# Down projections of a two-layer encoder: nine of sixteen feature pairs by a seven-product scheme in three groups, the last weights kept in SBUF

## The chip, the core and the metric

The kernel runs on one core of a Trainium2 chip. A core has a matrix engine (TensorE, PE in the profile; its weight loads are shown as PEld), a vector engine (VectorE, DVE), a scalar engine (ScalarE, ACT), a general engine (GpSimd, POOL) and a queue engine that only issues DMAs (SyncE, SP). They work from two on-chip memories, SBUF and PSUM (where matmuls accumulate, in eight banks), and each engine runs its own list of instructions in order, held up only by semaphores. DMA brings data from and to the chip's main memory. The metric is the device time of one execution, in microseconds, as the median of several runs; lower is better.

## What is computed

The reference is a trunk of two transformer layers, applied with the same weights to a batch of 512 tokens and one of 256, model width 1024, feed-forward width 4096, all in 32-bit floats. Layer 0 mixes neighbourhood attention and grouped-query attention, layer 1 is differential attention; each is followed by a squared-ReLU feed-forward block, and a norm ends the trunk:

```python
for layer in range(DEPTH):
    ...
    h = rmsnorm(x, ln_mlp[layer])
    x = x + jnp.square(jax.nn.relu(h @ w_up[layer])) @ w_down[layer]
return rmsnorm(x, ln_f)
```

The change is about the last product of each layer, `H @ w_down` with `H` of 768 tokens by 4096 features, called the down projection below.

## The kernel before

**Layout.** Activations are kept transposed: a tile has 128 features on the partitions and all 768 tokens (`NT`) along the free axis, the 512 tokens of one request first, the 256 of the other behind. `x`, the residual stream, is eight such tiles. `HT` is half the tokens, 384.

**Split operands.** A 32-bit product is made of three matmuls in the `fp32r` type: each operand is split into a high part, a copy rounded by ScalarE, and a low part, the rest, by a VectorE subtraction (`halve` for activations, lines 113 to 120; `wsplit` for weights, lines 77 to 82), and high x high, high x low and low x high are summed in PSUM. `wtile` loads a weight tile (three `wraw` buffers, by SP's queue) and splits it into `whi` and `wlo` (four buffers each).

**The feed-forward block** is `mlp` (line 798). The up projection already works by a seven-product scheme for 2 x 2 blocks of (128 output features) x (512 input features) x (384 tokens): `weights` loads a block pair and has POOL form four sums of weight blocks (line 866), `second` forms the sums of activations once (lines 822 to 838), `product` (line 874) issues 12 matmuls of 384 columns for each of the seven products, and VectorE adds the results into `z` (line 889 and its neighbours). `finish` applies norm, ReLU and square and writes each pair of 128 features, `H[mp]`, to DRAM; there are sixteen pairs in a layer.

**The down projection** follows (lines 960 to 991). It runs in `NG` = 4 groups of `GF` = 8 feature tiles, that is, four pairs. For each group `read` (line 919) loads a pair of `H` into an `hr` tile (two buffers, issued on POOL's queue, line 922) and splits it into two `hp` tiles. Then, for each of four output pairs `mq`, two weight tiles are loaded and split, and for each of two output tiles `m`, `proj_feat` (line 195, its matmul on line 204) issues 8 x 3 x 2 matmuls: eight feature tiles, three terms, and two pieces of the tokens, of 512 columns (`dna`, a bank with the tag `mm`) and 256 columns (`dnb`, tag `at`). VectorE adds the two banks to `x[m]` (line 982). There are three `mm` and five `at` banks.

The last group of layer 1 is `final` (line 769): it runs over the 512-token piece and then over the 256-token piece, loading and splitting the group's eight weight tiles for each piece anew, and after each piece it does the last norm (`rstd`, `spread`), scales the eight tiles by `R` on VectorE and POOL (line 795) and writes the output. In layer 0 the last group also splits the new `x` for the next layer and sums its squares.

**What sets the order.** The kernel is written for a tile framework that follows the program's dependencies, hands out buffers of each tag, places the semaphores, and arranges each engine's list of instructions when the kernel is built: an instruction written later may be placed earlier where its inputs and buffers allow. On the chip the order of each engine's list is then fixed.

## Time and profile before

| what | value |
|---|---|
| median of 3 runs | 1823.96 us (1821.44 to 1826.17) |
| the profiled execution's own time | 1822.1 us |
| its span in the profile | 1820.1 us |
| mean granted clock of TensorE | 0.992 |
| first down projection's matmuls | from 621.2 to 892.7 us |
| second down projection, `final` included | from 1533.8 to 1809.2 us |

The profile is one execution. A row of a group of instructions gives source line, engine, operation, output and input by the program's names, shapes and count, then the busy time and the mean duration of one, then the idle time of that engine just before these instructions and what ended it. Matmuls overlap one another, so that a matmul's duration is longer than the distance between two starts. Timeline rows give the start in microseconds from the span's start, the duration, and the instruction. A line number can be that of a helper: line 81 is the low part of any weight, line 117 that of any activation without a gain.

### The profile page before, as it was taken

How to read it: one execution, taken by the hardware profiler on the slowest of the kernel's cores; microseconds unless marked ns; L12 is line 12 of the kernel's file. 1: busy time of each engine (PE TensorE's matmuls, PEld its weight loads, DVE VectorE, ACT ScalarE, POOL GpSimd, SP SyncE). 2: the span in 40 equal slices, each digit the busy share in tenths (PEclk: the TensorE clock that was granted, in tenths of full speed). 3: DMA queues.
4: the chain of work that ended last, by engine and by line, in shares of the span. 5: the costliest groups of instructions: out<-in, count | busy, mean ns of one | idle time of the engine just before them, and what ended most of it. 6: DMA issues, size and time to landing. Idle time of an engine off the chain costs nothing.

```text
span 1820.1 us, 28502 instructions
## 1 busy us (share of the span) xinstructions
PE 1777.1 (98%) x11358; PEld 1627.3 (89%) x11358; DVE 1127.7 (62%) x2083; ACT 764.2 (42%) x1485; POOL 363.5 (20%) x366
## 2 busy tenths in 40 slices
PE   7999999999999999999999999999989999999997
PEld 7877888899999988888999999988989999888877
DVE  7777647497766634325366776775976667343255
ACT  6665534364434412213235555554544334122143
POOL 1421000014544200000022222210235442000002
PEclk8999999999999999999999999999999999999999
DMA  5111222313333634323211110122133336343233
GB/s 166 44 33 37 68 83 88 131 35 110 139 125 130 213 111 139 119 67 122 93 51 44 47 48 22 53 68 93 36 109 140 122 125 207 126 131 124 70 99 115
DMA packets 50019, 176.70 MB, mean 97 GB/s; under 512 B 5856, under 2 KB 8672, under 8 KB 49888
## 3 DMA queue, kind: packets, MB, share of 16 engines
q1 hardware_dynamic: 38656, 121.91, 21.2%
q0 software_dynamic: 4608, 25.17, 4.1%
q10 hardware_dynamic: 6624, 27.81, 3.9%
q8 instruction: 89, 1.46, 0.3%
q14 instruction: 42, 0.34, 0.1%
HBM read 142.63 MB, written 31.46 MB: 96 GB/s over the span
## 4 chain that ended last, share of the span: by engine, by line
PE 78%; DVE 8%; issue 8%; DMA 3%; ACT 3%; POOL 1%; DVEq 0%; SPq 0%; ACTq 0%; POOLq 0%
PE up L881 23%; PE dna L204 11%; PE dqk L192 8%; PE dnb L204 6%; PE opa L204 5%; PE dvp L192 4%; PE fin L786 3%; DMA hr<-H 2%; PE opb L204 2%; PE npa L204 2%; PE ds L270 2%; PE dpv L713 2%; DVE t L815 1%; PE vp L192 1%; PE qp L192 1%
## 5 line engine op out<-in xcount | busy, mean ns | idle before, releaser
L881 PE MATMUL up<-c,whi 128*128 128x384 f32 x1824 | 468.6, 338 | 5.8 <-ACT whi L80 5.8
L881 PEld LDWEIGHTS up<-c,whi 128*128 128x128 f32 x1824 | 331.9, 189 | 6.6 <-ACT whi L80 6.5
L204 PE MATMUL dna<-hp,whi 128*128 128x512 f32 x896 | 331.8, 394 | 1.1 <-DVE hp L117 0.9
L80 ACT ACTIVATE whi<-wraw 128x1024 fp32r<-128x1024 f32 (+2 forms) x200 | 193.3, 967 | 324.5 <-PE dnb L204 222.6
L881 PE MATMUL up<-c,wlo 128*128 128x384 f32 x912 | 308.1, 339 | 2.1 <-DVE wlo L81 2.1
L81 DVE TENSOR_TENSOR wlo<-wraw,whi 128x1024 fp32r<-128x1024 f32 (+2 forms) x204 | 228.4, 1121 | 98.9 <-ACT whi L80 98.7
L204 PE MATMUL dnb<-hp,whi 128*128 128x256 f32 x896 | 250.0, 283 | 0.0
L204 PEld LDWEIGHTS dna<-hp,whi 128*128 128x128 f32 x896 | 168.1, 188 | 42.1 <-DVE hp L117 1.9
L866 POOL TENSOR_TENSOR s<-wraw 128x512 f32<-128x512 f32 x56 | 94.1, 1699 | 414.9 <-DMA wraw<-in_w_up_dram 199.8
L204 PE MATMUL dna<-hp,wlo 128*128 128x512 f32 x448 | 176.6, 394 | 0.0
L881 PEld LDWEIGHTS up<-c,wlo 128*128 128x128 f32 x912 | 172.2, 189 | 2.9 <-DVE wlo L81 2.9
L204 PEld LDWEIGHTS dnb<-hp,whi 128*128 128x128 f32 x896 | 167.2, 188 | 0.3
L889 DVE TENSOR_TENSOR z<-up,z 128x384 f32<-128x384 f32 x168 | 92.9, 553 | 90.4 <-PE up L881 79.0
L982 DVE TENSOR_TENSOR x<-dna,x 128x512 f32<-128x512 f32 x56 | 38.7, 691 | 165.6 <-PE dna L204 165.4
L204 PE MATMUL dnb<-hp,wlo 128*128 128x256 f32 x448 | 126.9, 283 | 0.0
L192 PE MATMUL dqk<-whi,xh 128*128 128x256 f32 x384 | 114.7, 299 | 0.0
L192 PE MATMUL dqk<-whi,xl 128*128 128x256 f32 x384 | 107.5, 280 | 0.0
L192 PE MATMUL dqk<-wlo,xh 128*128 128x256 f32 x384 | 107.2, 279 | 0.0
L922 POOL DMA_DIRECT2D hr<-H x32 | 17.6, 550 | 431.6 <-DVE hp L117 390.8
L204 PEld LDWEIGHTS dna<-hp,wlo 128*128 128x128 f32 x448 | 84.1, 188 | 18.3
L80 ACT ACTIVATE whi<-s 128x1024 fp32r<-128x1024 f32 x56 | 59.5, 1063 | 84.8 <-PE up L881 83.5
L116 ACT ACTIVATE hp<-hr 128x768 fp32r<-128x768 f32 x64 | 50.9, 837 | 100.2 <-PE dnb L204 61.8
(214 smaller groups left out, 3892.7 us busy)
## 6 DMA issues: line engine op xcount, KB each, us to landing
wraw<-in_w_down_dram SPq DMA_DIRECT2D x72, 512.0 KB, 3.6
wraw<-in_w_up_dram SPq DMA_DIRECT2D x64, 512.0 KB, 3.5
H<-z ACTq DMA_DIRECT2D x32, 768.0 KB, 3.3
hr<-H POOLq DMA_DIRECT2D x32, 768.0 KB, 5.9
wraw<-in_w_in_o_dram SPq DMA_DIRECT2D x24, 512.0 KB, 3.6
wraw<-in_w_in_e_dram SPq DMA_DIRECT2D x16, 512.0 KB, 3.7
x<-in_xT_dram SPq DMA_DIRECT2D x16, 384.0 KB, 5.4
nbias<-in_bias_dram SPq DMA_DIRECT2D x20, 256.0 KB, 3.8
```

The source lines that it names most:

```text
L80: nc.scalar.activation(hi, raw, AF.Copy)
L81: nc.vector.tensor_tensor(out=lo, in0=raw, in1=hi.bitcast(F32), op=ALU.subtract)
L116: nc.scalar.activation(hi, src, AF.Copy)
L192: nc.tensor.matmul(ps[:, :256], st[:, tk], col(k, part, 0, 256), start=(k == 0 and i == 0), stop=(k == KD - 1 and i == 2))
L204: nc.tensor.matmul(ps[:, : e - s], w, mv[:, s:e], start=(k == 0 and i == 0), stop=(k == nk - 1 and i == 2))
L270: nc.tensor.matmul(out[h], q(a_, hp, qs), k(b_, hp, ks), start=i == 0, stop=i == 2)
L713: nc.tensor.matmul(pv, pt[:, i * P : (i + 1) * P], v[:, k0 // P + i, vc], start=(i == 0), stop=(i == nk - 1))
L786: nc.tensor.matmul(ps, lhs(k, part), mv[:, sl], start=(k == 0 and j == 0), stop=(k == GF - 1 and j == 2))
L866: nc.gpsimd.tensor_tensor(out=d_, in0=x_, in1=y_, op=ALU.add)
L881: nc.tensor.matmul(ps, part[a_][:, base + k * P : base + (k + 1) * P], t[:, b_], start=q + k + i == 0, stop=q == n - 1 and k == 3 and i == 2)
L889: nc.vector.tensor_tensor(out=out, in0=x_, in1=y_, op=op)
L982: evac_halves(pa, pb, lambda ps, s: nc.vector.tensor_tensor(out=xm[:, s], in0=ps, in1=xm[:, s], op=ALU.add))
```

## The change

Each down projection is cut by a plan of pairs: 2 plain, 3 by the seven-product scheme, 2 plain, 3, 1 plain, 3, 2 plain. The plain stretches work as before, with stretches of two pairs or one in place of four.

In a group of three pairs, each pair is a 2 x 2 block (two feature tiles by two token halves), and with two output tiles `q` (a 2 x 2 block of weights) gives seven products of 384 columns, each summed over the three pairs (`SJ`). `pair` loads a pair of `H`, forms four sums of its blocks on VectorE, and splits seven operands: three of 384 columns (`small`, buffers `c3`) and two of 768 columns that hold two operands each (`large`, buffers `c6`); `slot` hands out twelve of the first and eight of the second in turn. `down_weights` loads two weight tiles of 768 columns, has POOL form four sums, and splits four tiles. `down_pair` issues the products in the order 1, 2, 6, 5, 7, 3, 4 into three banks: `u` collects products 1, 6, 7 and 4, `v` collects 5 and 3, `r` holds 2. Between the products VectorE adds the current content of a bank to a half tile of `x` or subtracts it, seven times, and the next product goes on accumulating in the same bank. Weights are laid out for this on the host.

`H` is loaded by SP's queue in halves into four buffers of the tag `h`, which the block operands `c0` of the up projection used before. The two temporary weight sums of the up projection get a pool of their own (`us`), which is closed in the last step of the up projection; the sums of the down projection take a spare `x` tile (`sa`) and a tile in `pa_` (`sb`). In layer 0 the pool of split tiles for the next layer is opened after the last group of three.

`final` now has the plan's last stretch, two pairs. Its four weight tiles are loaded and split in the first token piece and kept for the second.

```diff
+SJ = 3
+PLAN = ((2, 0), (3, 1), (2, 0), (3, 1), (1, 0), (3, 1), (2, 0))
...
-        start = woff["w_down"]
         acc = cpool.tile([P, NT], F32, tag="acc", name="acc", bufs=1)
         R = cpool.tile([P, NT], F32, tag="R", name="R", bufs=1)
+        kept = []
         for i, (s, e) in enumerate(SEGS):
-            woff["w_down"] = start
             sl = slice(s, e)
             nm = Norm(sq, (s, e), acc)
             for mq in range(KD // 2):
-                ws = [wtile("w_down", 1024) for _ in range(2)]
+                if i == 0:
+                    kept.append([wtile("w_down", 1024)])
+                ws = kept[mq]
                 for mi in range(2):
                     m = 2 * mq + mi
                     ps = ps_tile("mm", "fin")[:, : e - s]
                     lhs = down_lhs(ws, mi)
-                    for k in range(GF):
+                    for k in range(len(hs)):
                         for j, (part, mv) in enumerate(((0, hs[k][0]), (0, hs[k][1]), (1, hs[k][0]))):
                             nc.tensor.matmul(ps, lhs(k, part), mv[:, sl], start=(k == 0 and j == 0),
-                                             stop=(k == GF - 1 and j == 2))
+                                             stop=(k == len(hs) - 1 and j == 2))
...
+        g1s, g2s, st, ms, bs, uss = (ExitStack() for _ in range(6))
+        hrp = st.enter_context(tc.tile_pool(name=f"hr{layer}", bufs=4, reuse_waits="tile"))
...
+            t = comb[c, j] = pool.tile([P, 2, HT], F32R, tag=f"c{c}" if c else "h", name=f"c{c}", bufs=4)
...
+                put(g1 if c else hrp, c, j, x[k][:, tk], gcol(g, k))
...
+        up = g2s.enter_context(tc.tile_pool(name="up", bufs=3, side="right", reuse_waits="tile"))
         g2 = g2s.enter_context(tc.tile_pool(name="g2", bufs=4, side="right", reuse_waits="tile"))
-        up = g2s.enter_context(tc.tile_pool(name="up", bufs=3, side="right", reuse_waits="tile"))
+        us = uss.enter_context(tc.tile_pool(name="us", bufs=3, side="right", reuse_waits="tile"))
...
+            sa, sb = (us.tile([P, 1024], F32, tag="s", name="s", bufs=3) for _ in range(2))
...
-        def read(pool, f):
-
-            hr = pa_.tile([P, 2, NT], F32, tag="hr", name="hr", bufs=2)
-            nc.gpsimd.dma_start(hr, H[f // 2])
+        ops = {}
+
+        def load(mp):
+            hr = [hrp.tile([P, NT], F32, tag="h", name="hr", bufs=4) for _ in range(2)]
             for i in range(2):
-                hp = pool.tile([P, 2, NT], F32R, tag="hp", name="hp")
-                halve(hp[:, 0], hp[:, 1], hr[:, i])
-                hs.append((hp[:, 0], hp[:, 1]))
+                nc.sync.dma_start(hr[i], H[mp][:, i])
+            return hr
+
+        def read(mps, places):
+            hs = []
+            for mp in mps:
+                hr = load(mp)
+                for i in range(2):
+                    pool, tag, bufs = places.pop(0)
+                    if tag == "c3":
+                        hi, lo = (pool.tile([P, 2, HT], F32R, tag=tag, name="c3", bufs=bufs).rearrange("p a t -> p (a t)") for _ in range(2))
+                    else:
+                        hp = pool.tile([P, 2, NT], F32R, tag=tag, name="hp", bufs=bufs)
+                        hi, lo = hp[:, 0], hp[:, 1]
+                    halve(hi, lo, hr[i])
+                    hs.append((hi, lo))
+            return hs
+
+        used = {3: 0, 6: 0}
+
+        def slot(n):
+            i = used[n]
+            used[n] += 1
+            if n == 3:
+                pool, bufs = (pa_, 5) if i % 12 < 5 else (ph_, 7)
+            else:
+                pool, bufs = (pm_, 3) if i % 8 < 3 else (ph_, 5)
+            return pool.tile([P, 2, HT * n // 3], F32R, tag=f"c{n}", name=f"c{n}", bufs=bufs)
+
+        def pair(mp):
+
+            eng = nc.vector
+            hr = load(mp)
+            b11, b12, b21, b22 = hr[0][:, A], hr[0][:, B], hr[1][:, A], hr[1][:, B]
+            t = pa_.tile([P, 3, HT], F32, tag="t", name="dt", bufs=1)
+            n6, n7, t4 = (t[:, i] for i in range(3))
+
+            def small(src, scale=None):
+                c = slot(3)
+                halve(c[:, 0], c[:, 1], src, scale)
+                return c[:, 0], c[:, 1]
+
+            def large(src):
+                c = slot(6)
+                halve(c[:, 0], c[:, 1], src)
+                return [(c[:, 0, h], c[:, 1, h]) for h in (A, B)]
+
+            d = ops[mp] = {1: small(b12, -1.0)}
+            eng.tensor_tensor(out=n7, in0=b11, in1=b21, op=ALU.subtract)
+            eng.tensor_tensor(out=b11, in0=b12, in1=b11, op=ALU.subtract)
+            eng.tensor_tensor(out=n6, in0=b21, in1=b11, op=ALU.add)
+            eng.tensor_tensor(out=t4, in0=b22, in1=n6, op=ALU.subtract)
+            d[3], d[2] = large(hr[1])
+            d[6], d[7] = large(t[:, :2].rearrange("p a t -> p (a t)"))
+            d[5] = small(b11)
+            d[4] = small(t4)
+
+        def down_weights():
+
+            w = SJ * P
+            raws = []
+            for _ in range(2):
+                raw, loads = wload("w_down", 2 * w)
+                loads[0]()
+                raws.append(raw)
+            a11, a22, a12, a21 = (r[:, i * w : (i + 1) * w] for r in raws for i in range(2))
+            sa = xo_tile("s")
+            sb = pa_.tile([P, NT], F32, tag="s", name="s", bufs=1)
+            s2, s1, s3, s4 = (r[:, i * w : (i + 1) * w] for r in (sa, sb) for i in range(2))
+            out = {}
+            for ps_, t in (((1, 4), raws[0]), ((2,), raws[1]), ((6, 5), sa), ((7, 3), sb)):
+                if t is sa:
+                    for d_, x_, y_ in ((s1, a21, a22), (s2, s1, a11), (s3, a11, a21), (s4, a12, s2)):
+                        nc.gpsimd.tensor_tensor(out=d_, in0=x_, in1=y_, op=ALU.add)
+                hi, lo = whilo(w * len(ps_))
+                wsplit(hi, lo, t[:, : w * len(ps_)])
+                for i, p in enumerate(ps_):
+                    out[p] = (hi, lo), i * w
+            return out
+
+        def down_pair(mps, q, w):
+
+            xs1, xs2 = x[2 * q], x[2 * q + 1]
+            x11, x12, x21, x22 = xs1[:, B], xs1[:, A], xs2[:, B], xs2[:, A]
+            u, v, r = ps_tile("at", "du")[:, :HT], ps_tile("at", "dv")[:, :HT], ps_tile("mm", "dr")[:, :HT]
+
+            def prod(ps, n, start):
+                part, base = w[n]
+                for j, mp in enumerate(mps):
+                    c = ops[mp][n]
+                    for i, (a_, b_) in enumerate(((0, 0), (0, 1), (1, 0))):
+                        nc.tensor.matmul(ps, part[a_][:, base + j * P : base + (j + 1) * P], c[b_],
+                                         start=start and j + i == 0, stop=j == SJ - 1 and i == 2, skip_group_check=not start)
+
+            def put(xd, ps, op=ALU.add):
+                nc.vector.tensor_tensor(out=xd, in0=xd, in1=ps, op=op)
+
+            prod(u, 1, True)
+            put(x11, u, ALU.subtract)
+            prod(r, 2, True)
+            prod(u, 6, False)
+            put(x11, r)
+            put(x12, u, ALU.subtract)
+            prod(v, 5, True)
+            prod(u, 7, False)
+            put(x22, v, ALU.subtract)
+            put(x22, u)
+            prod(v, 3, False)
+            put(x12, v)
+            prod(u, 4, False)
+            put(x21, u)
...
+                uss.close()
                 g1s.close()
                 pa_ = g1s.enter_context(tc.tile_pool(name=f"dna{layer}", bufs=4, reuse_waits="tile"))
-                read(pa_, 0)
-                read(pa_, 2)
+                hs = read(range(PLAN[0][0]), [(pa_, "hp", 4)] * 4)
...
-        pb_ = st.enter_context(tc.tile_pool(name=f"dnb{layer}", bufs=6, reuse_waits="tile"))
-        nxt, nn = [], Norm(sq)
-        for grp in range(NG):
-            if grp:
-                hs = []
-            for f in range(len(hs), GF, 2):
-                read(pa_ if grp and f in (2, 4) else pb_, grp * GF + f)
-            if layer == 1 and grp == NG - 1:
-                final(hs, x, sq)
-                st.close()
-                g1s.close()
-                return
+        pm_ = ms.enter_context(tc.tile_pool(name=f"dnm{layer}", bufs=3, reuse_waits="tile"))
+        ph_ = bs.enter_context(tc.tile_pool(name=f"dnh{layer}", bufs=3, reuse_waits="tile"))
+
+        def plain_down(hs, then):
+
             for mq in range(KD // 2):
-                ws = [wtile("w_down", 1024) for _ in range(2)]
+                ws = [wtile("w_down", min(len(hs), 4) * 256) for _ in range((len(hs) + 3) // 4)]
                 for mi in range(2):
                     m = 2 * mq + mi
                     pa, pb = ps_tile("mm", "dna"), ps_tile("at", "dnb")
-                    run(proj_feat(down_lhs(ws, mi), hs, GF, pa, pb))
+                    run(proj_feat(down_lhs(ws, mi), hs, len(hs), pa, pb))
                     xm = x[m]
                     evac_halves(pa, pb, lambda ps, s: nc.vector.tensor_tensor(out=xm[:, s], in0=ps, in1=xm[:, s], op=ALU.add))
-                    if grp == NG - 1:
-                        nxt.append(split(xm, "x", gcol(G_O, m)))
-                        nn.add(xm)
-        spill = dram.tile([P, KD, NT], F32, name="spill")
-        for m in range(KD):
-            nc.sync.dma_start(spill[:, m, :], x[m])
+                    then(xm, m)
+
+        plain_down(hs, lambda xm, m: None)
+        at = PLAN[0][0]
+        for n, pairs in PLAN[1:-1]:
+            mps = range(at, at + n)
+            at += n
+            if pairs:
+                w = down_weights()
+                for mp in mps:
+                    pair(mp)
+                for q in range(KD // 2):
+                    down_pair(mps, q, down_weights() if q else w)
+            else:
+                plain_down(read(mps, [(pa_, "hp", 4)] * 4), lambda xm, m: None)
+        hs = read(range(at, FF // 256), [(pa_, "hp", 4)] * 4)
+        bs.close()
+        es, nxt, nn = None, [], None
+        if layer == 1:
+            final(hs, x, sq)
+        else:
+            es, nn = open_hl(), Norm(sq)
+
+            def then(xm, m):
+                nxt.append(split(xm, "x", gcol(G_O, m)))
+                nn.add(xm)
+
+            plain_down(hs, then)
+            spill = dram.tile([P, KD, NT], F32, name="spill")
+            for m in range(KD):
+                nc.sync.dma_start(spill[:, m, :], x[m])
+        ms.close()
+        g1s.close()
         st.close()
-        g1s.close()
-        return es, nxt, nn, spill
+        if layer == 0:
+            return es, nxt, nn, spill
...
-    d["w_down"] = wd.transpose(0, 1, 5, 2, 4, 3, 6).reshape(-1)
+    parts = []
+    for l in range(2):
+        wd = i["w_down"][l].reshape(FF // 256, 2, P, D // 256, 2, P)
+        at = 0
+        for n, pairs in PLAN:
+            blk = wd[at : at + n]
+            at += n
+            for q in range(D // 256):
+                if pairs:
+                    for ij in (((0, 0), (1, 1)), ((0, 1), (1, 0))):
+                        parts.append(np.stack([blk[:, kh, :, q, m] for m, kh in ij]).transpose(2, 0, 1, 3).reshape(-1))
+                else:
+                    parts.append(blk[:, :, :, q].reshape(-1, min(2 * n, 4), P, 256).transpose(0, 2, 1, 3).reshape(-1))
+    d["w_down"] = np.concatenate(parts)
```

7 lines of the change are left out of this document (removed).

## The prediction

> **What bounds the kernel now.** I read the page's head and busy table first, then its chain of work that ended last, then the groups of instructions kept apart by shape, the stage windows, and the timelines at the ends of stages.
>
> ```profile
> span 1820.1 us, 28502 instructions
> PE 1777.1 (98%) x11358; PEld 1627.3 (89%) x11358; DVE 1127.7 (62%) x2083; ACT 764.2 (42%) x1485; POOL 363.5 (20%) x366
> ...
> PE 78%; DVE 8%; issue 8%; DMA 3%; ACT 3%; POOL 1%; DVEq 0%; SPq 0%; ACTq 0%; POOLq 0%
> ...
> L204 PE MATMUL dna<-hp,whi 128*128 128x512 f32 x896 | 331.8, 394 | 1.1 <-DVE hp L117 0.9
> ```
>
> PE is busy 98% of the span and is 78% of the chain; in the down projection (`dna`) it sits idle 1.1 us in all. So what counts there is how many matmuls PE issues and how fast. Busy time doesn't give the pace, because matmuls overlap; starts do.
>
> ```profile
> 611.80 0.51 PE L881 MATMUL up<-c,whi 128*128 128x384 f32 x2
> ...
> 621.19 0.39 PE L204 MATMUL dna<-hp,whi 128*128 128x512 f32 x1
> ...
> 885.72 0.39 PE L204 MATMUL dna<-hp,whi 128*128 128x512 f32 x1
> ...
> 892.74 0.28 PE L192 MATMUL dvp<-whi,xh 128*128 128x256 f32 x1
> ```
>
> The first two rows are the last 54 half-size products of the up projection: 9.39 us, so **0.1739 us per 384-column matmul**. The last two rows span the last 40 plain matmuls of layer 0, which alternate 512 and 256 columns: 7.02 us, **0.1755 us** each. The whole stage holds 1536 of them (16 pairs x 2 blocks x 8 rows x 3 terms x 2 token pieces) from 621.19 to 892.74: 271.55 us, only 2.0 us above 1536 x 0.1755.
>
> **The change part by part.** *What goes.* A plain feature pair costs 96 matmuls, 16.85 us. Three pairs cost 288, 50.54 us. In the new form one group takes, for each of 4 output pairs, 7 products x 3 pairs x 3 terms = 63 matmuls, so 252 x 0.1739 = 43.82 us. Saved per group 6.72 us; three groups in each of two layers give **-40.3 us**. The 512- and 256-column columns of `final` are only redistributed, since 4 pairs there become 2.
>
> *What VectorE gains.* The new work is all of kinds that the trace has.
>
> ```profile
> L81 DVE TENSOR_TENSOR wlo<-wraw,whi 128x768 fp32r<-128x768 f32 x16 | 15.2, 948 | 0.9 <-ACT whi L80 0.9
> L117 DVE TENSOR_TENSOR hp<-hr,hp 128x768 fp32r<-128x768 f32 x64 | 58.8, 954 | 46.1 <-ACT hp L116 45.7
> ...
> 605.74 1.22 DVE L81 TENSOR_TENSOR wlo<-s,whi 128x1024 fp32r<-128x1024 f32 x1
> 606.87 0.55 DVE L952 SCALAR_TENSOR_TENSOR z<-up,z 128x384 f32<-128x384 f32 x1
> 607.34 0.55 DVE L889 TENSOR_TENSOR z<-up,z 128x384 f32<-128x384 f32 x1
> 607.80 0.69 DVE L81 TENSOR_TENSOR wlo<-wraw,whi 128x512 fp32r<-128x512 f32 x1
> 608.40 0.55 DVE L889 TENSOR_TENSOR z<-up,z 128x384 f32<-128x384 f32 x1
> ...
> 671.83 0.69 DVE L982 TENSOR_TENSOR x<-dna,x 128x512 f32<-128x512 f32 x1 [2.13 <-PE dna L204]
> 672.44 0.41 DVE L982 TENSOR_TENSOR x<-dnb,x 128x256 f32<-128x256 f32 x1
> 672.77 1.22 DVE L81 TENSOR_TENSOR wlo<-wraw,whi 128x1024 fp32r<-128x1024 f32 x1
> ```
>
> Start to start, a queued VectorE instruction takes some 0.08 us less than its duration: 0.47 us for 384 columns, 0.60 for 512, 1.13 for 1024, 0.94 for an eviction of 512 plus 256, and so 0.87 for 768. Then:
> - `pair`: two 768-wide low parts, three 384-wide ones and four sums: 2 x 0.87 + 7 x 0.47 = 5.0 us, 15.1 for a group.
> - weights of one output pair: 3 x 0.87 + 0.47 = 3.1 us, 12.3 for a group.
> - seven `put`s of 0.47 us for each output pair: 13.2 for a group.
>
> A group so has 40.6 us of VectorE work beside 43.8 of PE. A plain stretch of two pairs has 4 x 0.87 + 4 x 1.13 + 8 x 0.94 = 15.5 of 33.7, one of a single pair 2 x 0.87 + 4 x 0.60 + 8 x 0.94 = 11.7 of 16.85. Per layer that is 180 us of VectorE beside 250 of PE: 72%. Is such a share harmless? The up projection already runs at it:
>
> ```profile
> 416.00:621.00 205.00, 205.00 (x1181) 205.00 (x1180) 143.25 (x170) 84.11 (x88) 91.77 (x51) 1.00 0.40 138
> 688.00:756.00 68.00, 68.00 (x389) 59.58 (x388) 24.13 (x32) 14.65 (x17) 1.91 (x4) 1.00 0.31 102
> ...
> L881 PE MATMUL up<-c,whi 128*128 128x384 f32 x1824 | 468.6, 338 | 5.8 <-ACT whi L80 5.8
> ```
>
> In the first window (columns: length, then busy of PE, PE loads, VectorE, ScalarE, POOL) VectorE is busy 143 of 205 us, 70%, and PE is busy throughout. In a plain down stage (second row) it was busy 24 of 68. So on average the added work is covered; what can show is where the share runs above that.
>
> *Starts of the groups.* The first product of a group needs `b12` of all three pairs, so all three must be nearly split when PE arrives. In the list they stand behind the evictions of the plain stretch before, but the built order is not the list's:
>
> ```profile
> 680.87 0.41 DVE L982 TENSOR_TENSOR x<-dnb,x 128x256 f32<-128x256 f32 x1
> 682.31 3.06 DVE L117 TENSOR_TENSOR hp<-hr,hp 128x768 fp32r<-128x768 f32 x3 [1.03 <-ACT hp L116]
> 685.36 1.23 DVE L81 TENSOR_TENSOR wlo<-wraw,whi 128x1024 fp32r<-128x1024 f32 x1
> 686.50 0.95 DVE L117 TENSOR_TENSOR hp<-hr,hp 128x768 fp32r<-128x768 f32 x1
> 688.68 0.69 DVE L982 TENSOR_TENSOR x<-dna,x 128x512 f32<-128x512 f32 x1 [1.23 <-PE dna L204]
> ```
>
> Group 0 began at 621.19 and 67.4 us of matmuls end it near 688.6, so 688.68 is its last eviction; four `hp` splits of the next group ran ahead of it. Splits are pulled forward into gaps as buffers allow. Buffers then decide. `slot` keeps 12 small and 8 large operands for a group's 9 and 6: one pair can be made ahead, two wait for the group before to finish.
> - First groups: in the 33.7 us of the opening stretch VectorE has 15.5 of its own, some 3.6 of the up projection's end, 3.1 of weights, 15.1 of pairs, less 1.7 done earlier: 35.6. Late by 2; bounds 0 and 5 (one pair). I take 2 x 2 = 4 us.
> - Second groups: 15.5 + 3.1 + 10.1 = 28.7 in 33.7 us: nothing; at most one more pair, 5.
> - Third groups, behind a single pair: 11.7 + 3.1 + 10.1 = 24.9 in 16.85: 8 late at worst, 0 if the small operands are made as the second group's last products free them. The first output pair consumes them over 10.9 us, so I take 3, for two layers 6 us.
>
> *The added wait.* `u` and `v` are evicted and then accumulated on: four times per output pair PE must wait for a `put`, 96 in all; every later matmul is queued behind it.
>
> ```profile
> 1809.06 0.28 PE L786 MATMUL fin<-hp,wlo 128*128 128x256 f32 x1
> 1809.38 0.42 DVE L788 TENSOR_TENSOR x<-fin,x 128x256 f32<-128x256 f32 x1 [1.51 <-PE fin L786]
> ...
> 1796.29 1.21 DVE L81 TENSOR_TENSOR wlo<-wraw,whi 128x1024 fp32r<-128x1024 f32 x1
> ...
> 1797.55 0.39 PE L786 MATMUL fin<-hp,wlo 128*128 128x256 f32 x1 [0.56 <-DVE wlo L81]
> ```
>
> Matmul end to VectorE start is 0.04 us (1809.34 to 1809.38), VectorE end to PE start 0.05 (1797.50 to 1797.55). A release therefore comes 0.34 + 0.04 + 0.55 + 0.05 = 0.98 us after the last matmul starts. One other product lies between, 10 starts or 1.74 us: 0.76 us of slack, nearly the length of a 768-wide split. Only a `put` that finds such a split just begun, or two instructions ahead, is late. Nothing if never, 0.2 us each (18) if usually; nearest to the up projection's 5.8 us for a whole stage, I take 2 us.
>
> *Tail and the rest.* The second piece of `final` halves to 96 matmuls of 256 columns, 11.4 us, without weight splits. But the first piece's scaling runs beside it:
>
> ```profile
> 1788.92 0.69 DVE L182 COPY R<-pb 128x512 f32<-128x512 f32 x1 [2.37 <-PE pb L180]
> 1789.65 6.38 DVE L795 TENSOR_TENSOR x<-x,R 128x512 f32<-128x512 f32 x5
> 1795.96 0.41 DVE L788 TENSOR_TENSOR x<-fin,x 128x256 f32<-128x256 f32 x1
> ```
>
> For 6.4 us no eviction runs and three `mm` banks hold three outputs, now 1.4 us each: about 2 us exposed beyond today's, between -2 and 5. ScalarE gains about as many splits but was busy 42% of the span, and stays below VectorE. H moves from POOL's queue to SP's, 64 loads of 384 KB in place of 32 of 768, ahead of weights in one queue:
>
> ```profile
> wraw<-in_w_down_dram SPq DMA_DIRECT2D x72, 512.0 KB, 3.6
> ...
> hr<-H POOLq DMA_DIRECT2D x32, 768.0 KB, 5.9
> ```
>
> Landing takes 3.6 to 5.9 us and a group lasts 44, so I cost it at nothing; if a load that waits for its buffer held a weight back, one landing per stretch, 14 x 3.6 = 50 us, would be the other end. POOL's 96 sums hide behind the next output pair.
>
> *Sum.* The profiled execution took 1822.1 us (span 1820.1 and 2.0 around it), 1.9 below the median 1823.96 of the runs. 1822.1 - 40.3 + 4 + 6 + 2 + 2 = 1795.8, and against the median **1797.7 us**.
>
> **A rule against it.** POOL's sums and VectorE meet already:
>
> ```profile
> L894 DVE SCALAR_TENSOR_TENSOR z<-z,R x32: 1744/2270/2852, 433.3 to 1539.2; 128x1536 f32<-128x1536 f32 x32
> L866 POOL TENSOR_TENSOR s<-wraw x56: 1292/1738/2627, 385.3 to 1505.1; 128x512 f32<-128x512 f32 x56
> ```
>
> The same VectorE instruction took 1744 to 2852 ns, its POOL neighbour 1292 to 2627. The Trainium skill, "SBUF — State Buffer", section "SBUF: two separate sides", says that a VectorE instruction with two SBUF inputs and a POOL instruction that reads SBUF take one port pair in turn, and that the loser waits out the other's whole instruction. The stretched durations agree. By that rule the new splits and sums stand still during POOL's 16 sums of a group, which is the first rival's mechanism.
>
> **The rivals.**
> 1. *VectorE falls behind.* At 1292 x 384/512, some 1.0 us each, 16 POOL sums in a group would leave 43.8 - 16 - 12.3 - 13.2 = 2.3 us for pairs, so all three fall into the plain stretch. After two pairs that fits (18.2 us free); after the single pair 5.2 are free for 18.2: 13 late, 10 felt, in place of 3 in each layer: 1812 us. For: the durations above. Against: they stretch some instructions only, and the 70% share of the up projection with the same sums cost PE almost nothing.
> 2. *The hand-overs eat the gain.* If the fixed VectorE order puts one more instruction before every `put`, the 0.76 us are used up and each costs 0.3 us: 28 in place of 2, 1824 us: no change. Against: evictions follow their matmuls at once in the rows above.
> 3. *Slower: the pairs are not made ahead.* Only four `hr` buffers, a single `t` and one spare set of slots. If two of three pairs are made with PE standing, each group loses 10.1 us, 60 in place of 10: 1848 us. It decides from about 6 us per group (40.3 less tail and hand-overs, over 6). Against: the rows at 682 to 688; and the freed slots come while a whole plain stretch is still to run.
> 4. *Everything is hidden*: 1822.1 - 40.3 + 1.9 = 1784.
>
> **How the numbers follow.** My forecast, 1788 to 1807: 0.56. Nearly all kept, 1780 to 1788: 0.10. First rival, 1807 to 1818: 0.17. Second, no change: 0.07. Third: 0.10. A measurement of this kernel can tell 0.3%, 5.5 us, from no change. So faster 0.83, within 0.3% 0.07, slower 0.10. The range 1783 to 1818 holds the first three cases, except the lowest end, and leaves out the last two: the upper bounds of all unknown costs together belong to those.
>
> **What would show it.** 1428 down matmuls per layer in place of 1536, the half-size ones 0.174 us apart; group starts with PE waiting for `c3` or `c6` by 2 to 3 us in the first and third groups and hardly in the second; no long total of PE waits for the `put`s; VectorE busy around 72% of the down stages; four times 1.4 us of matmuls held up in the last 20 us. I'd be wrong if PE waits in every group for operands, if SP shows weights behind H loads, or if the half-size pace is slower than in the up projection.

## The result and the profile after

The changed kernel takes 1799.09 us (median of 4 runs, 1796.12 to 1800.31) against 1822.7 us before (median of 4): 0.9868 of it, 95% interval 0.9854 to 0.9883. The forecast was 1797.7 us. The profiled execution took 1799.98 us, with a span of 1798.2 us, 21.9 us less than before.

Lines moved: in the changed kernel 1018 is the matmul of a group, 1022 a `put`, 975 to 978 the four sums of `pair`, 1000 POOL's sums of weight blocks, 83 and 119 the low parts of weights and activations, 791 and 798 the last evictions and scalings. From the page, its head, the chain, two groups of instructions and two rows of the DMA table:

```profile
span 1798.2 us, 28909 instructions
PE 1745.1 (97%) x11142; PEld 1630.2 (91%) x11142; DVE 1322.0 (74%) x2433; ACT 818.1 (45%) x1595; POOL 476.1 (26%) x430
...
PE 80%; DVE 14%; ACT 3%; issue 2%; POOL 1%; DMA 0%; DVEq 0%; SPq 0%; ACTq 0%; POOLq 0%
...
L1018 PE MATMUL du<-c,whi 128*128 128x384 f32 x576 | 148.8, 340 | 10.2 <-DVE x L1022 10.2
...
hr<-H SPq DMA_DIRECT2D x64, 384.0 KB, 3.6
wraw<-in_w_down_dram SPq DMA_DIRECT2D x48, 384.0 KB, 3.2
```

PE issues 216 matmuls fewer (11358 before), as six groups of 36 should save. VectorE's part of the chain has grown from 8% to 14%. Before the matmuls of the groups into `u` PE stood idle 10.2 us, and all of it, twelve waits, ended with a `put`, none with an operand. The loads on SP's queue land in 3.2 to 3.6 us, and PE waits for none of them (the first sums of `pair` wait for `H` by 3.5 us in all).

The stages of layer 0, by windows cut at the first matmul of each stretch and group (columns: length, then busy time and instructions of PE, PE loads, VectorE, ScalarE and POOL, granted clock, DMA share, GB/s):

```profile
622.34:656.03 33.69, 33.69 (x193) 29.53 (x193) 33.23 (x54) 14.65 (x21) 9.88 (x6) 1.00 0.57 177
656.03:705.46 49.43, 45.49 (x254) 44.03 (x253) 46.23 (x68) 21.54 (x31) 15.13 (x11) 1.00 0.46 137
705.46:739.17 33.71, 33.71 (x193) 29.54 (x193) 28.98 (x44) 10.02 (x16) 6.84 (x6) 1.00 0.38 109
739.17:783.54 44.37, 44.37 (x254) 44.30 (x253) 31.51 (x50) 16.54 (x24) 12.73 (x10) 1.00 0.28 88
783.54:800.40 16.86, 16.86 (x98) 14.77 (x97) 16.78 (x29) 5.77 (x10) 6.93 (x5) 1.00 0.51 158
800.40:846.33 45.93, 44.79 (x254) 44.18 (x253) 34.17 (x51) 14.28 (x18) 14.94 (x11) 1.00 0.27 80
846.33:880.03 33.70, 33.70 (x193) 29.54 (x193) 24.97 (x33) 16.12 (x19) 0.00 (x0) 1.00 0.48 165
```

The plain stretches are exactly as costed. The groups took 49.43, 44.37 and 45.93 us where 43.82 was the ideal; in layer 1 they took 49.46, 44.38 and 45.95. The first group of a layer, not the third, is the late one, and that is where VectorE is busy 46.2 us.

By the timelines, from the first matmul of each down projection to the first matmul behind it (in layer 1 that of the norm behind `final`). Before, the second one starts at 1532.91 us, not at the 1533.8 of the table ahead of the prediction:

| stage | before | after | difference |
|---|---|---|---|
| layer 0, down projection | 271.55 | 257.69 | -13.86 |
| layer 1, down projection with `final` | 276.27 | 266.62 | -9.65 |
| everything else | 1272.3 | 1273.9 | +1.6 |
| span | 1820.1 | 1798.2 | -21.9 |

The 16.8 us between the -40.3 of the matmuls and the -23.5 of the two stages have to be explained. The late `put`s look like this in the timeline of the first group. First three PE rows (in brackets the idle time before, and what ended it), then VectorE's rows over 7 us, then POOL's in the same time:

```profile
676.41 0.59 PE L1018 MATMUL du<-c,whi 128*128 128x384 f32 x2 [1.25 <-DVE x L1022]
...
685.46 0.59 PE L1018 MATMUL du<-c,whi 128*128 128x384 f32 x2 [0.91 <-DVE x L1022]
...
689.59 0.58 PE L1018 MATMUL du<-c,whi 128*128 128x384 f32 x2 [0.72 <-DVE x L1022]
```

```profile
681.97 1.18 DVE L976 TENSOR_TENSOR hr<-hr 128x384 f32<-128x384 f32 x1
683.08 1.77 DVE L83 TENSOR_TENSOR wlo<-s,whi 128x768 fp32r<-128x768 f32 x1
684.77 0.54 DVE L1022 TENSOR_TENSOR x<-x,du 128x384 f32<-128x384 f32 x1
685.24 1.11 DVE L977 TENSOR_TENSOR dt<-hr 128x384 f32<-128x384 f32 x1
686.39 1.26 DVE L978 TENSOR_TENSOR dt<-hr,dt 128x384 f32<-128x384 f32 x1
687.57 0.54 DVE L1022 TENSOR_TENSOR x<-x,dr 128x384 f32<-128x384 f32 x1
688.04 0.95 DVE L83 TENSOR_TENSOR wlo<-wraw,whi 128x768 fp32r<-128x768 f32 x1
```

```profile
681.73 1.01 POOL L1000 TENSOR_TENSOR s<-wraw 128x384 f32<-128x384 f32 x1 [7.21 <-DVE wlo L83]
682.82 1.22 POOL L1000 TENSOR_TENSOR s<-s,wraw 128x384 f32<-128x384 f32 x1
684.93 1.01 POOL L1000 TENSOR_TENSOR s<-wraw 128x384 f32<-128x384 f32 x1 [0.90 <-DVE wlo L83]
685.89 1.34 POOL L1000 TENSOR_TENSOR s<-wraw,s 128x384 f32<-128x384 f32 x1
```

The same 768-wide split took 1.77 us beside POOL's sums and 0.95 without; the 384-wide sums took 1.1 to 1.26 us, twice what an undisturbed one takes. The `put`s, which read PSUM, are not stretched. The `put` at 684.77 had to wait for the stretched split, and PE for the `put`.

### The profile page after: what moved, and what is told of

It is laid out like the page before. It is cut to its first block, busy times and chain, and to the rows that moved or that the text cites. A ratio compares the mean times of both kernels' runs of the same rounds, so it can differ in the third digit from the quotient of the medians.

```text
span 1798.2 us, 28909 instructions
## 1 busy us (share of the span) xinstructions
PE 1745.1 (97%) x11142; PEld 1630.2 (91%) x11142; DVE 1322.0 (74%) x2433; ACT 818.1 (45%) x1595; POOL 476.1 (26%) x430
## 4 chain that ended last, share of the span: by engine, by line
PE 80%; DVE 14%; ACT 3%; issue 2%; POOL 1%; DMA 0%; DVEq 0%; SPq 0%; ACTq 0%; POOLq 0%
PE up L886 24%; PE dqk L194 8%; PE du L1018 7%; PE opa L206 5%; PE dna L206 5%; PE dvp L194 4%; PE dv L1018 4%; PE opb L206 2%; PE npa L206 2%; PE dnb L206 2%; DVE wlo L83 2%; DVE c L119 2%; PE ds L272 2%; PE dpv L715 2%; PE fin L789 2%
## 5 line engine op out<-in xcount | busy, mean ns | idle before, releaser
L82 ACT ACTIVATE whi<-wraw 128x1024 fp32r<-128x1024 f32 (+3 forms) x208 | 180.0, 867 | 185.5 <-PE dv L1018 49.1
L83 DVE TENSOR_TENSOR wlo<-wraw,whi 128x1024 fp32r<-128x1024 f32 (+3 forms) x212 | 211.6, 1000 | 24.4 <-ACT whi L82 23.1
L82 ACT ACTIVATE whi<-s 128x1024 fp32r<-128x1024 f32 (+1 forms) x104 | 100.1, 963 | 167.1 <-PE up L886 86.6
L1018 PE MATMUL du<-c,whi 128*128 128x384 f32 x576 | 148.8, 340 | 10.2 <-DVE x L1022 10.2
L206 PE MATMUL dna<-hp,whi 128*128 128x512 f32 x384 | 142.3, 392 | 0.0
L83 DVE TENSOR_TENSOR wlo<-s,whi 128x1024 fp32r<-128x1024 f32 (+1 forms) x104 | 124.7, 1199 | 22.3 <-ACT whi L82 21.7
L1018 PEld LDWEIGHTS du<-c,whi 128*128 128x128 f32 x576 | 103.2, 188 | 14.7 <-ACT whi L82 7.5
L206 PE MATMUL dnb<-hp,whi 128*128 128x256 f32 x384 | 108.7, 283 | 0.0
L1018 PE MATMUL du<-c,wlo 128*128 128x384 f32 x288 | 96.9, 338 | 0.0
L206 PEld LDWEIGHTS dna<-hp,whi 128*128 128x128 f32 x384 | 72.1, 188 | 16.8
```

The lines of the kernel that those rows point to most:

```text
L82: nc.scalar.activation(hi, raw, AF.Copy)
L83: nc.vector.tensor_tensor(out=lo, in0=raw, in1=hi.bitcast(F32), op=ALU.subtract)
L206: nc.tensor.matmul(ps[:, : e - s], w, mv[:, s:e], start=(k == 0 and i == 0), stop=(k == nk - 1 and i == 2))
L1018: nc.tensor.matmul(ps, part[a_][:, base + j * P : base + (j + 1) * P], c[b_], start=start and j + i == 0, stop=j == SJ - 1 and i == 2, ski ...
```

## The experiments

Theory: the groups lose because POOL's sums stretch VectorE's instructions, and a stretched instruction ahead of a `put` uses up more than the slack that the `put` has. Rivals: VectorE simply has too much to do; the splits wait for POOL's results; operands of a group, or splits for a later stretch, stand in the wrong order. Each kernel ran once, e11 five times, beside the kernel before on the same chip, whose span was 1817.9 to 1825.5 us there. The start of the first down projection moves between 618 and 623 us from run to run with the up projection before it, so groups are compared by their own lengths, and differences of 3 us between spans say little.

| run | span | groups of layer 0 | groups of layer 1 |
|---|---|---|---|
| changed kernel | 1798.2 | 49.43, 44.37, 45.93 | 49.46, 44.38, 45.95 |
| e2, no sums on POOL | 1782.0 | 44.3 to 44.4 | 44.3 to 44.4 |
| e3, own banks | 1785.1 | 44.4 | 44.4 |
| e4, splits held | 1793.5 | 45.34, 47.94, 45.89 | 44.97, 47.70, 46.16 |
| e5, one later, last stretch short | 1805.0 | 47.91, 44.35, 45.79 | 47.71, 44.38, 45.83 |
| e6, one later, second stretch short | 1800.9 | 45.75, 47.98, 45.95 | 45.69, 47.98, 45.94 |
| e9, sums unread | 1802.5 | 52.36, 44.37, 47.43 | 47.51, 44.78, 46.92 |
| e10, sums on VectorE | 1781.3 | 44.39, 44.36, 44.37 | 44.48, 44.36, 44.43 |
| e12, sums on both | 1816.5 | 50.63, 48.48, 49.83 | 51.69, 49.96, 49.26 |

**e1: no groups at all.** Only the plan is changed back to plain stretches.

```diff
-PLAN = ((2, 0), (3, 1), (2, 0), (3, 1), (1, 0), (3, 1), (2, 0))
+PLAN = ((2, 0),) * 8
```

> The plan is eight plain stretches of two pairs: the new buffers, SP loads, kept weights and doubled number of evictions, without any group of seven products. If the gain is all the groups' fewer matmuls (my step: 40.3 us of PE, some 17 us lost again in the groups, 5 in the tail), the span comes back to that of before, 1815 to 1822 us, with 11358 matmuls and no PE wait for a put. If the rest of the change had its own share of the gain, the span lies clearly under 1812; if it cost something, above 1824.

It had a span of 1824.3 us beside 1819.6 for the kernel before, one execution each. Its two down projections took 269.6 and 279.4 us, 549.0 in all, where the kernel before took 547.8. The loads by SP, the smaller stretches and the kept weights bring nothing by themselves; the whole gain is the groups'.

**e2: POOL's sums left out.** The splits that read sums read the raw weights.

```diff
-            for ps_, t in (((1, 4), raws[0]), ((2,), raws[1]), ((6, 5), sa), ((7, 3), sb)):
-                if t is sa:
-                    for d_, x_, y_ in ((s1, a21, a22), (s2, s1, a11), (s3, a11, a21), (s4, a12, s2)):
-                        nc.gpsimd.tensor_tensor(out=d_, in0=x_, in1=y_, op=ALU.add)
+            for ps_, t in (((1, 4), raws[0]), ((2,), raws[1]), ((6, 5), raws[0]), ((7, 3), raws[1])):
```

> Leaves out POOL's four sums of weight blocks in each output pair of a group: the raw weights are split in their place, with the same number and width of splits. Theory A (VectorE is full from the start of the stage, and splits for later stages stand in its order ahead of the puts): the first groups stay near 48 to 49 us, the third near 46. Theory B (POOL's sums hold the shared port and stretch VectorE's instructions to 1.3 to 1.8 us): no VectorE instruction of a group is stretched any more, the waits for puts from the second output pair on are gone, first groups at 45 to 46.5, third at 44.5, span 8 to 11 us less than 1798.

All six groups came down to 44.34 to 44.37 us, the first ones further than either theory expected, and no `put` was waited for. So the sums are at the root of the lateness, and the operands' place in the order is not. VectorE, with the same 2433 instructions, was busy 1294.7 us in place of 1322.0: the stretching costs it 27.3 us. What is left over 43.82 is the pace: 44.36 / 252 = 0.1760 us per matmul, where the last 54 matmuls of the up projection gave 0.1739.

**e3: a bank for every product.** No product goes on in a bank that a `put` has still to read; the sums over products are not formed in PSUM.

```diff
-            prod(u, 1, True)
-            put(x11, u, ALU.subtract)
-            prod(r, 2, True)
...
+            for n, tag, puts in ((1, "at", ((x11, ALU.subtract),)), (2, "mm", ((x11, ALU.add),)), (6, "at", ((x12, ALU.subtract),)),
...
+                ps = ps_tile(tag, f"d{n}")[:, :HT]
+                prod(ps, n, True)
```

> Each of the seven products starts afresh in a bank of its own and is added once, so that no product waits for a put of the one before; the number and size of VectorE instructions stays (the accumulation over products is left out). If the loss of the groups is the hand-over (a put that comes late stops PE at once), all groups take 43.8 to 44.5 us and the span falls by 10 to 12 us. If VectorE simply has too much to do there, PE waits for free banks instead and the first groups stay above 47.

The groups took 44.34 to 44.36 us although POOL's sums were all there and VectorE was still stretched (busy 1320.2 us). One sum of `pair` in this run, and the same in e2 without POOL's sums (columns: duration in ns, least, median and most, first and last start):

```profile
L977 DVE TENSOR_TENSOR dt<-hr x18: 541/558/1265, 638.6 to 1684.0; 128x384 f32<-128x384 f32 x18
```

```profile
L977 DVE TENSOR_TENSOR dt<-hr x18: 546/557/560, 633.0 to 1679.8; 128x384 f32<-128x384 f32 x18
```

So here stretching harms only through the hand-over: with a spare bank PE doesn't feel it.

**e4: splits of the next plain stretch held back** until the third output pair's last `put`, to take them out of the first group.

```diff
-                plain_down(read(mps, [(pa_, "hp", 4)] * 4), lambda xm, m: None)
+                with tc.issue_after(held[2]):
+                    hs = read(mps, [(pa_, "hp", 4)] * 4)
+                plain_down(hs, lambda xm, m: None)
```

> The splits of H for the plain stretch behind a group are queued on VectorE behind the last put of the group's third output pair, otherwise all as in the change. Theory A: the four hp splits leave the first output pair of the first groups (3.5 to 4 us of VectorE work), the two or three waits of that pair shrink from 2.8 us to under 1, first groups 46 to 47.5 us, span 4 to 7 us less. Theory B: no change in the waits from the second output pair on and less than 1 us in all.

The first groups gained 4.1 and 4.5 us, the second ones lost 3.6 and 3.3: in all 139.2 and 138.8 us where it had been 139.7 and 139.8. The lateness only moved. The span's 4.7 us less are for the most part an earlier start of the down projection.

**e5 and e6: the groups later in the layer**, so that VectorE has one more plain pair to get ahead in.

```diff
-PLAN = ((2, 0), (3, 1), (2, 0), (3, 1), (1, 0), (3, 1), (2, 0))
+PLAN = ((2, 0), (1, 0), (3, 1), (2, 0), (3, 1), (1, 0), (3, 1), (1, 0))
...
-                    kept.append([wtile("w_down", 1024)])
+                    kept.append([wtile("w_down", len(hs) * 256)])
```

> Plain stretches of 2+1, 2, 1, 1 pairs in place of 2, 2, 1, 2: the first group comes 16.9 us later, final has one pair. If the first group's 5.6 us of waiting come from VectorE being full since the end of the up projection, they go: first groups 44.4 to 45.5 us in both layers (10 us less in all), second 44.4, third near 46 as before. Final: the pieces are 11.2 and 5.7 us of matmuls beside the same 6.3 us of scaling, so that 5 us or so come back in layer 1. Rival (POOL contention is per group, wherever it stands): first groups stay over 47.

In e6 the second group, too, stands behind a single pair, and `final` has two pairs as in the changed kernel: (2, 0), (1, 0), (3, 1), (1, 0), (3, 1), (1, 0), (3, 1), (2, 0).

> Plain stretches of 2+1, 1, 1, 2 pairs: the first group comes 16.9 us later, the second behind a single pair, final as in the change. By the VectorE account: first groups 44.4 to 45.5 us, second and third 46 each (a single pair leaves 5 us for 15 us of pairs), 3 to 4 us less per layer. If the room ahead of a group doesn't matter, all as in the change: 49.4, 44.4, 46.

e5's first groups gained 1.5 to 1.8 us, not more, its opening three pairs took 53.0 us where 50.55 is the ideal, and `final`, with one pair, lost at the end. e6 moved part of the lateness to the second groups (47.98 us), and its three groups took 139.7 us as before. Neither gained. A longer run-up is no remedy while VectorE is stretched all the way.

**e7: the last weights not kept**, but loaded and split again for the second piece of tokens.

```diff
-        kept = []
+        start = woff["w_down"]
...
-                if i == 0:
-                    kept.append([wtile("w_down", 1024)])
-                ws = kept[mq]
+                if mq == 0:
+                    woff["w_down"] = start
+                ws = [wtile("w_down", 1024)]
```

> Final loads and splits its four weight tiles again for the second piece of tokens, as before the change. The second piece gets 4 x 1.13 us of VectorE work and four loads. If that piece is bound by VectorE (6.3 us of scaling with PE waiting 3.8 us behind it), its 20.3 us grow by 2 to 5 us; if it is bound by the banks alone, by less than 1. Everything before it is unchanged.

The second piece, from its first matmul to the norm's, took 20.93 us where it had been 20.28: the kept weights are worth 0.65 us, under the 1 us expected if the banks alone bind this piece.

**e8: the scaling of the first piece spread** between the second piece's evictions. `scaled` holds the scaling and the output of one tile, which stood in a loop behind each piece before; the last two tiles follow behind the second piece's last eviction.

```diff
...
+                    if i and m >= 2:
+                        scaled(m - 2, slice(*SEGS[0]))
+            if i:
+                for k in (6, 7):
+                    scaled(k, slice(*SEGS[0]))
...
```

> The scaling of the first token piece is written between the evictions of the second piece (one tile behind each from the third on), in place of all at once before them. If the wait of 3.8 us in final comes from five scalings in a row on VectorE with three mm banks full, it shrinks to under 1.5 us and the second piece takes 17 to 18.5 us in place of 20.3; the last scaling may come later by up to 2 us. If VectorE's total decides, the wait only changes its place and the end stays within 1 us.

The second piece took 17.65 us, 2.6 less. In the changed kernel the timeline of the last stage shows why (VectorE, then PE; then the windows around it):

```profile
1774.29 6.29 DVE L798 TENSOR_TENSOR x<-x,R 128x512 f32<-128x512 f32 x5
...
1781.31 0.51 PE L789 MATMUL fin<-hp,whi 128*128 128x256 f32 x2 [3.61 <-DVE x L791]
```

```profile
1773.07:1777.50 4.43, 4.43 (x40) 4.43 (x38) 4.15 (x4) 0.42 (x1) 3.31 (x3) 1.00 0.17 63
1777.50:1781.31 3.81, 0.20 (x2) 0.00 (x1) 3.81 (x7) 0.53 (x2) 1.33 (x1) 1.00 0.90 347
1781.31:1785.00 3.69, 3.69 (x18) 3.69 (x19) 2.12 (x6) 2.92 (x7) 0.00 (x0) 0.55 0.36 139
```

Five scalings in one go keep PE waiting 3.6 us for a bank, and after the pause PE ran 3.7 us at a granted clock of 0.55, with 18 matmuls in it where 40 had taken 4.4 us.

**e9: POOL's sums formed, but read by nobody.** This tells stretching from waiting for POOL's results.

```diff
                 hi, lo = whilo(w * len(ps_))
+                t = {id(sa): raws[0], id(sb): raws[1]}.get(id(t), t)
                 wsplit(hi, lo, t[:, : w * len(ps_)])
```

> POOL forms its four sums as in the change, but the splits read the raw weights, so the sums are written and not used: the port stays shared, the dependence of the splits on POOL is gone. Port (theory B): VectorE's sums dt, hr still average 700 ns or more in place of 552, PE waits for puts 8 us or more in all, first groups 48 to 50 us. Dependence (rival: without sums the weight splits were only ready sooner): all groups 44.4 us as without sums, waits for puts under 1 us.

The waits stayed and even grew, from 10.2 to 12.0 us in all, and the groups took 283.4 us where it had been 279.5. The lateness fell differently on the two layers: the first groups took 52.36 and 47.51 us, both outside the 48 to 50 expected. Who waited for the `put`s of this run (us, times):

```profile
who waited for it (us, times):
  PE du L1019: 12.0, 7
  PEld du L1019: 6.3, 5
```

It is not the splits' dependence on the sums.

**e10: the sums on VectorE.** VectorE, the busy engine, gets 96 instructions more.

```diff
-                        nc.gpsimd.tensor_tensor(out=d_, in0=x_, in1=y_, op=ALU.add)
+                        nc.vector.tensor_tensor(out=d_, in0=x_, in1=y_, op=ALU.add)
```

> The four sums of weight blocks in the groups are formed by VectorE in place of POOL: 96 more VectorE instructions of some 0.47 us, 7.5 us for a group, and no POOL instruction that reads SBUF there. If stretched instructions alone make the puts late, the waits vanish and groups are at 44.4 to 45.5 us. If the sum of VectorE's work decides, the first groups (46.2 us of VectorE work, some 5 of it stretch) end with more of it than before and stay at 49 to 52 us, the third at 46 to 48, the second may rise to 45 to 47.

All groups took 44.36 to 44.48 us, 266.4 in all where it had been 279.5: 13.1 us. The page's busy row, and the windows of the first four stages (columns as above, cut 1 to 1.4 us behind each stage's first matmul):

```profile
PE 1737.5 (98%) x11142; PEld 1625.5 (91%) x11142; DVE 1335.7 (75%) x2529; ACT 819.3 (46%) x1595; POOL 343.9 (19%) x334
```

```profile
619.00:653.00 34.00, 34.00 (x196) 29.97 (x195) 33.12 (x58) 14.57 (x22) 0.00 (x0) 1.00 0.51 161
653.00:697.50 44.50, 44.50 (x254) 44.23 (x253) 42.94 (x72) 19.13 (x25) 0.00 (x0) 1.00 0.48 148
697.50:731.00 33.50, 33.50 (x193) 29.52 (x192) 32.10 (x58) 13.00 (x19) 0.00 (x0) 1.00 0.44 128
731.00:775.50 44.50, 44.50 (x255) 44.25 (x254) 35.29 (x60) 16.52 (x24) 0.00 (x0) 1.00 0.30 89
```

VectorE is busy 42.9 of 44.5 us in the first group, a greater share (96%) than in the changed kernel (94%), and PE is busy without a break. Too much VectorE work is therefore not the cause by itself. The 96 sums, at the 0.47 us from start to start that the prediction used, are 45 us, but VectorE's total rose by only 13.7: stretching had cost it about 31 us, by this estimate. The changed kernel's groups by shape show most of it:

```profile
L83 DVE TENSOR_TENSOR wlo<-s,whi 128x768 fp32r<-128x768 f32 x48 | 51.4, 1070 | 5.6 <-ACT whi L82 5.2
...
L83 DVE TENSOR_TENSOR wlo<-wraw,whi 128x768 fp32r<-128x768 f32 x40 | 40.0, 1001 | 2.4 <-ACT whi L82 1.4
...
L119 DVE TENSOR_TENSOR hp<-hr,hp 128x768 fp32r<-128x768 f32 x28 | 29.4, 1072 | 2.3 <-ACT hp L118 2.1
...
L977 DVE TENSOR_TENSOR dt<-hr 128x384 f32<-128x384 f32 x18 | 13.9, 770 | 0.3
...
L978 DVE TENSOR_TENSOR dt<-hr,dt 128x384 f32<-128x384 f32 x18 | 13.6, 758 | 0.1
L976 DVE TENSOR_TENSOR hr<-hr 128x384 f32<-128x384 f32 x18 | 13.5, 748 | 0.2
...
L975 DVE TENSOR_TENSOR dt<-hr 128x384 f32<-128x384 f32 x18 | 13.1, 726 | 3.7 <-DMA hr<-H 3.5
```

The 72 sums of `pair` are 14.5 us over 72 x 0.55, the 116 splits 10.6 us over 116 x 0.95: 25 us in these rows. In e10 all four sums have a median of 0.55 us and none is over 0.56.

**e12: the sums on VectorE, and POOL given as much work back** that nothing reads (1536 columns per output pair, as before the move); beside e10's edit it has the one below. VectorE's 2529 instructions stand in the same order in the traces of e10 and e12.

```diff
+                    for i in range(6):
+                        spare = pa_.tile([P, 256], F32, tag="sp", name="sp", bufs=1)
+                        third = slice(i % 3 * 256, i % 3 * 256 + 256)
+                        nc.gpsimd.tensor_tensor(out=spare, in0=raws[0][:, third], in1=raws[1][:, third], op=ALU.add)
```

> As e10 (the sums of weight blocks on VectorE), and POOL is given sums of the same size back, which nothing reads: per output pair six sums of 256 columns of the same two raw weight tiles into a spare tile, in place of four of 384. VectorE's own list is that of e10. Theory (POOL's and VectorE's instructions stretch each other, and a stretched split or sum ahead of a put is longer than the 0.76 us that a put may be late): the stretched durations come back (maxima of 1.2 us and more for the 384-wide sums of pairs instead of 0.56), PE waits for puts again, by 6 to 14 us in all, and the first groups last 46 to 50 us; the span is 1787 to 1798 us instead of 1781.3. Rival (it is the order in which VectorE was given its work in e10, or which engine makes the sums that the splits wait for, and not the stretching): all groups stay at 44.4 to 44.6 us and the span at 1780 to 1784 us.

The direction was right, the size was not: the groups took 299.8 us in all, 33.5 more than in e10, and the span was 1816.5 us, nearly the kernel before. The first group, the plain stretch behind it and the second group, to be read beside those of e10, and who waited for the `put`s:

```profile
653.02:703.65 50.63, 46.70 (x254) 45.48 (x253) 48.65 (x81) 21.07 (x29) 14.08 (x12) 0.97 0.43 134
703.65:737.36 33.71, 33.71 (x194) 29.55 (x193) 32.84 (x51) 12.95 (x20) 11.02 (x12) 1.00 0.40 120
737.36:785.84 48.48, 45.02 (x254) 44.06 (x253) 40.37 (x67) 16.55 (x24) 11.65 (x12) 1.00 0.28 83
```

```profile
who waited for it (us, times):
  PE du L1022: 19.8, 10
  PEld du L1022: 13.5, 6
```

Work on POOL that nobody waits for, with VectorE's order unchanged, brings the waits back. VectorE was already 92% busy over the four windows of e10 (143.5 of 156.5 us) and had no room for being stretched, so every group lost, the second too. The six largest waits, 2.2 to 3.3 us near the start of each group, have no stretched instruction right ahead of them. This is the one of the second group, with VectorE's instructions ahead of it (1088 is the eviction of a plain stretch here, 1026 a `put`):

```profile
743.88 0.59 PE L1022 MATMUL du<-c,whi 128*128 128x384 f32 x2 [3.20 <-DVE x L1026]
...
741.39 0.69 DVE L1088 TENSOR_TENSOR x<-dna,x 128x512 f32<-128x512 f32 x1
...
742.32 0.95 DVE L83 TENSOR_TENSOR wlo<-s,whi 128x768 fp32r<-128x768 f32 x1
743.18 0.56 DVE L1026 TENSOR_TENSOR x<-x,du 128x384 f32<-128x384 f32 x1
```

POOL's last sum had ended 18 us earlier, and all these instructions have their undisturbed lengths. But VectorE still evicted the plain stretch at 741.39, 4 us after PE had left it: what the stretching had cost before was carried along, and the first `put` of the group paid for it. POOL's reads also keep the raw weight tiles longer, but later weights explain little: PE waited 1.5 us for a `whi`. From the start of each down projection to the end of its last group VectorE was busy 35.8 us more than in e10 (430.3 and 394.5 us for both layers), its idle time fell from 40.4 to 38.1 us, and ScalarE's and VectorE's waits for weight loads were 8.6 us in e12 and 8.7 in e10.

**e11: both gains together**, the edits of e8 and e10.

> The changed kernel with two edits at once: the sums of weight blocks on VectorE (as in e10) and the scaling of the first piece written between the second piece's evictions (as in e8). Theory (the stretching of VectorE's and POOL's instructions by each other is what the groups lose, and the second piece's late scaling is a loss of its own): the two add up; every group lasts 44.3 to 44.5 us, no PE wait for puts, the second piece 17.6 to 17.8 us, so the profiled span is 1781.3 - 2.6 = about 1778.7 us, the time about 1780.5 us, 0.977 of the kernel before. Rival (VectorE, 96% busy in the first groups, has no room left, and what the tail gains is lost at the end of the last group): the span stays at 1781 us or above. No change expected anywhere outside the down stages.

1782.53 us (median of 5 runs, 1781.03 to 1785.76), 0.9779 of the kernel before, 95% interval 0.9759 to 0.9799; span 1779.2 us, second piece 17.78 us. The two add up to within 1 us, and its median is 16.6 us below that of the changed kernel. Not every group lasted 44.3 to 44.5 us as expected: the first of layer 1 took 45.09, with one wait of 0.37 us for a `put`. There no instruction was stretched; ScalarE had waited for loads of `H` and VectorE 1.2 us for ScalarE.

## Why the prediction was right

The total was right to 1.4 us, but several steps were off and partly made up for each other. Term by term, for the profiled execution:

| term | predicted | measured |
|---|---|---|
| 216 matmuls fewer, those of the groups at 0.1739 us | -40.3 | -40.3 |
| groups over 43.82 us: lateness and hand-overs | +12 | +16.6, of it 3.2 pace |
| second piece of `final`, beyond its matmuls and what it lost before | +2 | +4.9 |
| stalls of the kernel before that went | 0 | -4.6 |
| all other stages | 0 | +1.6 |
| sum | -26.3 | -21.8 |

The profiled spans differ by 21.9. The medians differ by 23.6, and against the median before the prediction's own difference was 26.3.

- **The matmuls.** The count and the form of the sum were right. The pace of the half-size matmuls was taken from the up projection; in groups it is 0.1760 us even without any stall, 0.54 us per group. About 0.2 of this is the choice of the sample: the 973 matmuls of that up projection from 451.26 to 621.01 us start 0.1746 us apart on average, and its last 54 are among the fastest. The rest is open.
- **Starts of the groups.** 10 us for operands not yet split was wrong in the mechanism: no wait ended with an operand. VectorE was behind at the start of the first groups, but through the stretching and not by the account of 35.6 in 33.7 us (in e2, without POOL's sums, nothing is late), and what it delayed was the last evictions of the plain stretch and then the group's first `put`s: 1.5 us in each first group and 1.6 in each third, 6.2 in all by the starts of the matmuls. "Nothing" for the second groups was right. That the first groups lost 5.1 us beyond the pace, close to the upper bound of 5 for this step, is chance, since the bound stood for a pair made late.
- **The hand-overs.** This is the step that failed: 2 us for 96 waits. Further on in the first groups the `put`s cost 3.5 us each, 7.1 in all; with those at the starts, late `put`s took 13.3 us. That 12 us forecast for both steps lie near it is luck. The slack of 0.76 us and what would use it up (a `put` that "finds such a split just begun, or two instructions ahead") were right, but durations of undisturbed instructions were used. Stretched ones of 1.1 to 1.8 us are longer than the slack, and what they cost VectorE before a group shows at the group's first `put`. Without POOL's sums (e2, e10), or with a bank to spare (e3), the hand-overs cost nothing.
- **The first rival** had the mechanism and the wrong consequence. I let POOL take away VectorE's time and so make pairs late behind the single plain pair; the third groups should have lost 10 us. What came was lateness at the `put`s, in the groups where VectorE is full: 46.2 of 49.4 us in the first and 31.5 of 44.4 in the second, which lost nothing although POOL worked 12.7 us there (15.1 in the first). The price was too high as well: a POOL sum costs VectorE about 0.3 us on average (27.3 us for 96, by e2) and not the 1.0 us that this rival set down. Stretching costs where VectorE has no room: e10 has no room and no stretching, the second group of the changed kernel both room and stretching, and neither loses.
- The Trainium skill, "SBUF — State Buffer", section "SBUF: two separate sides", has the loser wait out the other's instruction. The durations agree: a sum of `pair` of 0.55 us took at most 1.37, so 0.82 more, and the split of 0.95 at most 1.77, again 0.82 more, where POOL's sum takes 1.0 us at least. With POOL's narrower sums of e12, of 0.73 us at least, both took at most 0.55 us more. The Trainium skill's page "Perfetto Trace Analysis", section "Optimizing Scalar/DVE Operations", says that moving work between VectorE and POOL might not help. Here moving it back to the fuller engine gained 13.1 us.
- **VectorE's share** of the down projection was to be 72%; it was 84% in layer 0 (215.9 of 257.7 us). Stretching accounts for 13 to 16 us per layer, by e10; the rest was not taken apart.
- **The tail.** The place was right, the size too low: one wait of 3.6 us and then the low clock.
- **SP's queue at nothing** was right. The 4.6 us that I had not counted on are the boundaries of the kernel before: 2.0 over the ideal in layer 0, 0.5 and 2.1 in layer 1 (46.77 us for the first piece of `final`, twice 22.31 after).
- The third and the second rival fall: PE never stood for pairs, and not every `put` was late.

What is not shown is whether, in e10, the list that the framework built for VectorE with the sums in it helped as well. e12 keeps this order and loses, so that order alone is no protection.

## What to carry to other kernels

When work is moved to POOL to spare a busy VectorE, count what it does to VectorE's instructions with two SBUF inputs, in two ways. Look at the longest of them: what stands ahead of an eviction must be shorter than the eviction's slack. And add up what they lose where VectorE has little room: that lateness is carried along to the next eviction that PE waits for. A busy engine without surprises did better here than a less busy one whose instructions double in length now and then. Where a bank was read and then accumulated on, a bank for every product took the waits away (e3).

## What the runs showed of the hardware

- POOL's additions of 384 columns (1.0 us each alone) cost VectorE 25 to 31 us for 96 of them, about 0.3 us each (27.3 by e2). Given back in e12 as 144 of 256 columns, they cost it 35.8 us (1371.5 less 1335.7). The `put`s, with one input in PSUM, took 0.56 us at most beside them.
- A wait of PE of 3.6 us was followed by 3.7 us at a granted clock of 0.55. At the pace ahead of it (40 matmuls in 4.43 us) the 18 matmuls of this time would have taken 2.0 us, so the wait cost about 1.7 us beyond its own length.
- Matmuls of the same shape start every 0.1739 to 0.1754 us in the up projection (blocks of 54) and every 0.1760 us in the groups, at a granted clock of 1.00 in both. No run here tells why.
